# A 31-tap depthwise convolution: from VectorE taps to fp32 matrix products in four column groups

## The chip, the cores and the metric

The kernel runs on one core of one Trainium2 chip. The metric is the time of one execution on the device in microseconds (us), lower is better. The engines are called by the names that the profile uses: PE is TensorE's matrix products and PEld its weight loads, DVE is VectorE, ACT is ScalarE, POOL is GpSimd, and SP issues most of the DMAs. Each engine works through its instructions in the order in which they stand in its own queue.

## The reference

One layer of a hybrid diffusion backbone over T = 1024 tokens of width D = 1024. A modulated norm and one input projection give the inputs of four head groups of 256 channels: a Conformer convolution, a Fourier mixing (FNet), a neighbourhood attention and a state space model (SSM). Their outputs are normed, joined and projected, and a squared-ReLU MLP follows. Only the convolution is touched here:

```python
def conformer_conv(u, w_dw, b_dw, ln_g, ln_b, w_pw, b_pw):
    a, g = jnp.split(u, 2, axis=-1)
    v = a * jax.nn.sigmoid(g)
    v = lax.conv_general_dilated(v, w_dw[:, None, :], window_strides=(1,),
        padding=[(CONV_WIDTH // 2, CONV_WIDTH // 2)],   # 31 taps, 15 each side
        dimension_numbers=("NWC", "WIO", "NWC"),
        feature_group_count=D_GROUP) + b_dw             # 256 channels, one filter each
    v = jax.nn.silu(layernorm(v, ln_g, ln_b))
    return v @ w_pw + b_pw
```

## The kernel before

Everything is fp32. Most products split both factors in a high and a low part and take three products of them; the split of a tile is one ACT copy (`..h`) and one subtraction on DVE or POOL (`..l`). Activations lie with channels on the 128 partitions and tokens along the row, so that the 256 channels of the convolution are two blocks m = 0, 1 of 128, and the 1024 tokens two halves hf of H = 512 columns, one PSUM tile each.

The stages in time are: norms and modulation, the input projection with the SSM (to about 270 us), then a mixed stage to 400 us, the attention (from 400 us, 32 units to about 580), and the MLP to the end. The mixed stage holds the projection tiles of the convolution and of the queries (`x_tile`, 24 products of 512 columns each, L364), the SSM's output gate (GLU, `og` and `oa`), the FNet (`pz`, `pp`, `pq`, `fo`) and the group norms of their outputs (`pa` sums on PE, a square root and reciprocal `rc` on ACT and DVE, `pb` broadcasts on PE). The scheduler orders each engine's queue there. In the attention PE's order is written out by hand (`manual_schedule`): for each unit n the transposes of its probabilities (`p_t`, L1258), the scores of unit n + 2 (`p_s`, L1239 to L1242), from n = 4 on six steps of output-projection work (`fill(FILL)`), and the value products of unit n - 1 (`p_t`, L1270). Between `p_s` and `p_t` of a unit lie a DVE reduction (`pr`, L1244), an exponential on ACT (L1246) and, for the values, a copy on ACT (`ptt`). DVE and ACT take on these and all other work in the order that the scheduler gives.

The convolution itself: `conv_in(m)` makes the gated input in `cv` with 15 zeros on each side. `tap_steps(m, hf)` then makes one half of one block: of the 31 taps, seven are ACT scalings whose products POOL adds (`pacc`, L1013), 24 run on DVE, the first as a scaling with the bias (L1007), 23 as multiply and add (`cacc`, L1015), and a last DVE addition joins the two sums (L1018). The two halves of block 0 are called ahead of the attention, except the last two steps; those of block 1 are handed out inside it, nine steps a unit (`fill(TAPS, tps)`).

Of the kernel before, what the change touches and what calls it, by code (L numbers as in the profile page):

```python
# [8 lines left out]
F32 = mybir.dt.float32  # L9
# [8 lines left out]
P = 128  # L18
# [5 lines left out]
TWO_PI = 6.2831845  # L24
PI_ = 3.14159225
NQ = 190

COLS = {}
_n = 0
for _name, _w in (("b_mod", 48), ("g_mix", 8), ("g_mlp", 8), ("b_out", 8),  # L30
                  ("b_ff2", 8), ("g_group", 8), ("w_dw", 62), ("b_dw", 2),
                  ("ln_g", 2), ("ln_b", 2), ("b_pw", 2), ("b_fnet", 2), ("b_glu", 4),
                  ("ssm_d", 8), ("are", 16), ("aim", 16), ("cc", 16), ("g_final", 8), ("b_ff1", 32)):
    COLS[_name] = (_n, _w)
    _n += _w
# [1 line left out]
CST = {}  # L37
_n = 0
for _name, _w in (("ident", 128), ("bdc", 128), ("bds", 128), ("nidx", NQ), ("sel", 2), ("idk", 16),
                  ("rowm", 24), ("colm", 96)):  # L40
    CST[_name] = (_n, _w)
    _n += _w
NCST = _n
# [6 lines left out]
def body(tc, A, out, dbg=None):  # L50
# [60 lines left out]
    def C(name, i=0, n=1):  # L111
        o, w = COLS[name]
        return cols[:, o + i:o + i + n]
# [157 lines left out]
    kb = dram.tile([16, 16, 15, 16], F32, name="kb")  # L271
    ys_d = dram.tile([256, 8, P], F32, name="ys_d")
    yg_d = dram.tile([2, 2, P, T], F32, name="yg_d")

    st = ExitStack()
    p1 = open_pool("p1", "left", stack=st)
# [486 lines left out]

    cs = ExitStack()
    cp = open_pool("conv", "left", stack=cs)
    vs = []
    for m in range(2):
        v = cp.tile([P, T + 30], F32, name=f"cv{m}")
        V.memset(v[:, 0:15], 0.0)
        V.memset(v[:, T + 15:T + 30], 0.0)  # L770
        vs.append(v)
    wdw = cp.tile([P, 62], F32, name="wdw")
    V.tensor_scalar(wdw, C("w_dw", 0, 62), 0.5, None, ALU.mult)

    def conv_in(m):
        w = load_w(A["w_in"][2 + m])
        gth = [cp.tile([P, H], F32, name="cth", tag="csq", bufs=2) for _ in range(2)]
        for hf in range(2):
            S.activation(gth[hf], x_tile(w, hf), AF.Tanh, scale=0.5)
        w = load_w(A["w_in"][m])  # L780
        for hf in range(2):
            V.scalar_tensor_tensor(vs[m][:, 15 + hf * H:15 + (hf + 1) * H], gth[hf], 1.0, x_tile(w, hf),
                                   ALU.add, ALU.mult)

    sh = open_pool("shared", "left", stack=cs)
    ka = open_pool("keys", "left", stack=cs)
    gl = ExitStack()
    gp = open_pool("glu", "left", stack=gl)
    q4 = lambda name, dt=F32: sh.tile([P, T], dt, name=name, tag="q4", bufs=9)
    norms = []  # L790
    conv_in(0)

# [29 lines left out]
        norms.append((3, ths, [yg_d[1, m, :, sl] for m in range(2)]))  # L822
    for a_ in norms[-2:]:
        group_norm_d(gp, *a_)


    fwr = gp.tile([P, 2, 256], F32, name="fwr", tag="gsq", bufs=2)
# [163 lines left out]
    prep_bias(2)  # L991
    for jc in (0, 1, 3):
        bias(4 + jc)

    NP_TAPS = 7
    accs = [None, None]

    def tap_steps(m, hf):
        if hf == 0:
            accs[m] = cp.tile([P, T], F32, name="cacc", tag="c4", bufs=2)  # L1000
        o_ = hf * H
        acc = accs[m][:, o_:o_ + H]
        w = lambda k: wdw[:, m * 31 + k:m * 31 + k + 1]
        x = lambda k: vs[m][:, o_ + k:o_ + k + H]
        pacc = cp.tile([P, H], F32, name="pacc", tag="csq", bufs=2)
        S.activation(pacc, x(0), AF.Copy, scale=w(0))
        V.tensor_scalar(acc, x(NP_TAPS), w(NP_TAPS), C("b_dw", m), ALU.mult, ALU.add)  # L1007
        done = 1
        for n, k in enumerate(range(NP_TAPS + 1, 31)):
            if done < NP_TAPS and done * (30 - NP_TAPS) <= n * NP_TAPS:  # L1010
                t = cp.tile([P, H], F32, name="ptmp", tag="csq", bufs=2)
                S.activation(t, x(done), AF.Copy, scale=w(done))  # L1012
                G.tensor_tensor(pacc, pacc, t, ALU.add)  # L1013
                done += 1
            V.scalar_tensor_tensor(acc, x(k), w(k), acc, ALU.mult, ALU.add)  # L1015
            yield
        assert done == NP_TAPS
        V.tensor_tensor(acc, acc, pacc, ALU.add)  # L1018
        yield


    mods(1)
    for _ in tap_steps(0, 0):
        pass
    tap01 = tap_steps(0, 1)
    LATE, LD, H1 = 2, 1, 0
    for _ in range(31 - NP_TAPS - LATE):
        next(tap01)
    hps.close()


# [251 lines left out]
        yield from w_steps(0, 0)  # L1283
        yield from w_steps(2, 0)

    def taps():
        for hf in range(2):
            yield from tap_steps(1, hf)

    def mod_steps():  # L1290

        for i in range(mod_state[0], 32, 2):
# [24 lines left out]
    GL = {19: (3, 1, (0,)), 21: (3, 1, (1,)), 23: (1, 1, (0,)), 25: (1, 1, (1,))}  # L1317
    w_order = [2 * g + q for g in (3, 1, 0, 2) for q in range(2)]
    w_next = []
    bulk, tps = bulk_steps(), taps()  # L1320
    chains = {0: ln_steps(0), 1: ln_steps(1), 2: na_steps(0), 3: mod_steps()}
    TAPS = 9
    plan = {n: [] for n in range(NU)}
    for c, at in enumerate((LN0, LN1, NA0, MOD)):
        for n in at:
# [26 lines left out]
    with tc.manual_schedule(engines={mybir.EngineType.PE}):  # L1352
        scores(0)
        scores(1)
        with tc.issue_after(state["min", H1]):
            prep_head(1)
        with tc.issue_after(state["min", 1]):
            for _ in range(LATE):
                next(tap01)
        for q in range(8):  # L1360
            if LG[q] < 0:
                lead(q)
        w_next.append(load_w(A["w_out"][w_order.pop(0)]))
        for n in range(NU):
            with tc.issue_after(state["min", min(n + LD, NU - 1)]):
                for q in range(8):
                    if LG[q] == n:
                        lead(q)
            fill(TAPS, tps)
            transposes(n)  # L1370
            if n + 2 < NU:
                scores(n + 2)
            if n >= START:
                fill(FILL)
            if n > 0:
# [448 lines left out]
    return np.ascontiguousarray(v.reshape(-1, P).T)  # L1824


def ssm_d(d):
    o = np.zeros((2, 2, 32, 8), np.float32)
    o[:, :, :16] = d.reshape(8, 2, 16).transpose(1, 2, 0)
    return o.reshape(P, 8)  # L1830


def prep(inp):
# [21 lines left out]
        "b_mod": _colv(a["b_mod"][0]), "g_mix": _colv(a["g_norm_mix"][0]), "g_mlp": _colv(a["g_norm_mlp"][0]),  # L1855
        "g_final": _colv(a["g_final"]), "b_out": _colv(a["b_out"][0]), "b_ff1": _colv(a["b_ff1"][0]),
        "b_ff2": _colv(a["b_ff2"][0]), "g_group": _colv(a["g_group"][0]),
        "w_dw": a["conv_w_dw"][0].T.reshape(2, P, 31).transpose(1, 0, 2).reshape(P, 62),
        "b_dw": _colv(a["conv_b_dw"][0]), "ln_g": _colv(a["conv_ln_g"][0]), "ln_b": _colv(a["conv_ln_b"][0]),
        "b_pw": _colv(a["conv_b_pw"][0]), "b_fnet": _colv(a["fnet_b"][0]), "b_glu": _colv(a["ssm_b_glu"][0]),  # L1860
        "ssm_d": ssm_d(a["ssm_d"][0]),
# [16 lines left out]
def shape_constants():  # L1878
    c = {}
    k = np.arange(64)  # L1880
    ang = 2 * np.pi * ((k[:, None] * k[None, :]) % 64) / 64
    bd = np.zeros((2, P, P))
    for i in range(2):
        s = slice(64 * i, 64 * i + 64)
        bd[0, s, s] = np.cos(ang) / 256
        bd[1, s, s] = np.sin(ang) / 256
    nidx = np.zeros((P, NQ))
    nidx[:64] = np.arange(NQ)
    nidx[64:] = NQ - 1 - np.arange(NQ)
    sel = np.zeros((P, 2))  # L1890
    for q in range(4):
        for v in range(2):
            sel[32 * q + v, v] = 1
    idk = np.zeros((P, 16))
    for q in range(4):
        idk[32 * q:32 * q + 16] = np.eye(16)
    rowm = np.full((8, 16, 2, 12), 1e30)
    colm = np.full((8, 16, 3, 32), 1e30)
    for rh in range(2):
        for r in range(8):  # L1900
            r0 = min(max(8 * rh + r - 4, 0), 8) - 4 * rh
            rowm[r, :, rh, r0:r0 + 8] = 0
    for jc, (q0, kc0) in enumerate(((0, 0), (16, 8), (48, 32))):
        for cq in range(16):
            c0 = min(max(q0 + cq - 8, 0), 48) - kc0
            colm[:, cq, jc, c0:c0 + 16] = 0
    c["cst"] = np.concatenate([np.eye(P), bd[0], bd[1], nidx, sel, idk, rowm.reshape(P, 24), colm.reshape(P, 96)], axis=1)


    d = np.zeros((4, 2, P, 256))  # L1910
    tk = np.arange(256).reshape(2, P, 1)
    for i in range(2):
        n = 2 * tk + i
# [21 lines left out]
```

## Time and profile before

| what | value |
|---|---|
| three runs, median (lowest to highest) | 1340.45 us (1339.1 to 1341.78) |
| the profiled execution, own time | 1341.13 us |
| its span in the trace | 1339.0 us |
| mean granted TensorE clock | 0.947 of full speed |
| PE busy | 1197.4 us (89%) |
| DVE busy | 1068.4 us (80%) |
| POOL busy | 808.6 us (60%) |
| ACT busy | 652.7 us (49%) |

The span is the part of the execution that the trace covers, and 2.1 us lie around it. Busy shares are means over the stages. All times below are us from the start of the span.

### The profile page before, as it was taken

The numbers are of one execution on the slowest core, as the hardware profiler recorded it, in microseconds if no ns is written. First come the engines' busy times: TensorE is split into PE (matmuls) and PEld (weight loads), VectorE is DVE, ScalarE is ACT, GpSimd is POOL, SyncE is SP. The second block draws the span as 40 slices with busy tenths as digits, with TensorE's granted clock in tenths as the row PEclk, the third lists the DMA queues.
The fourth block names the chain that finished last, engine by engine and source line by source line (L and its number), as shares of the span: only waits on it lengthen the run. The fifth ranks groups of instructions, "written<-read, shape, count | busy, mean of one in ns | idle before, by whom it ended". The sixth has DMA issues, their size and how long they took to land.

```text
span 1339.0 us, 18718 instructions
## 1 busy us (share of the span) xinstructions
PE 1197.4 (89%) x6188; PEld 965.5 (72%) x6188; DVE 1068.4 (80%) x1636; ACT 652.7 (49%) x1337; POOL 808.6 (60%) x1002
## 2 busy tenths in 40 slices
PE   5889878898865999899999999999999999999996
PEld 3657656777655777777778777777877777777775
DVE  4775999869999768658695579888888888888867
ACT  5254333323446565554664445555545555444555
POOL 3825677372556734015367477777877778787754
PEclk9989898998975999898999999999999999999998
DMA  9455232161153544323121121111211112211113
GB/s 344 142 164 164 81 125 79 47 199 66 51 177 94 175 128 142 109 78 143 32 77 43 40 64 32 48 56 56 63 56 32 52 52 63 64 41 39 56 40 126
DMA packets 75058, 121.77 MB, mean 91 GB/s; under 512 B 16977, under 2 KB 35154, under 8 KB 74962
## 3 DMA queue, kind: packets, MB, share of 16 engines
q1 hardware_dynamic: 62802, 113.24, 26.9%
q10 hardware_dynamic: 12160, 7.34, 1.8%
q8 instruction: 49, 0.80, 0.3%
q14 instruction: 47, 0.39, 0.1%
HBM read 106.68 MB, written 13.88 MB: 90 GB/s over the span
## 4 chain that ended last, share of the span: by engine, by line
PE 48%; DVE 29%; ACT 5%; issue 4%; POOL 4%; DMA 3%; SPq 1%; ACTq 0%; DVEq 0%; POOLq 0%
PE fa L1472 11%; PE qa L1472 6%; PE qb L1472 5%; PE fb L1472 5%; DVE cacc L1015 5%; DVE tl L1488 3%; PE fc L1472 2%; DVE fl L1488 2%; PE f L1472 2%; PE p_t L1270 2%; PE mm L1097 2%; PE mm L1472 2%; DVE Ss L698 2%; DVE Ss L697 1%; DVE X L1493 1%
## 5 line engine op out<-in xcount | busy, mean ns | idle before, releaser
L1456 POOL TENSOR_TENSOR w2l<-w2r,w2h 128x128 fp32r<-128x128 f32 (+1 forms) x232 | 177.4, 766 | 75.3 <-ACT w2h L1455 68.1
L1493 DVE SCALAR_TENSOR_TENSOR X<-fa,gt2c,X 128x512 f32<-128x512 f32 x216 | 159.4, 745 | 13.0 <-PE fa L1472 13.0
L1455 ACT ACTIVATE w2h<-w2r 128x128 fp32r<-128x128 f32 (+1 forms) x232 | 85.8, 387 | 150.8 <-POOL w2r L1706 79.8
L1456 POOL TENSOR_TENSOR w2l<-w1r,w2h 128x256 fp32r<-128x256 f32 x136 | 108.5, 814 | 57.7 <-ACT w2h L1455 34.0
L235 POOL TENSOR_TENSOR wlo<-wraw,whi 128x1024 fp32r<-128x1024 f32 x30 | 75.2, 2508 | 102.0 <-ACT whi L233 82.9
L1493 DVE SCALAR_TENSOR_TENSOR X<-fb,gt2c,X 128x512 f32<-128x512 f32 x108 | 80.5, 745 | 35.4 <-PE fb L1472 35.3
L1456 POOL TENSOR_TENSOR w2l<-ws,w2h 128x256 fp32r<-128x256 f32 x84 | 67.9, 815 | 41.4 <-ACT w2h L1455 40.1
L1015 DVE SCALAR_TENSOR_TENSOR cacc<-cv,wdw,cacc 128x512 f32<-128x512 f32 x92 | 92.3, 1047 | 0.6
L364 PE MATMUL mm<-xl,whi 128*128 128x512 f32 x192 | 81.2, 424 | 3.8 <-DVE xl L220 3.8
L364 PE MATMUL mm<-xh,whi 128*128 128x512 f32 x192 | 77.3, 423 | 7.0 <-ACT xh L218 5.8
L1472 PE MATMUL fa<-th,w2h 128*128 128x512 f32 x156 | 63.2, 405 | 19.7 <-DVE X L1493 19.7
L364 PE MATMUL mm<-xh,wlo 128*128 128x512 f32 x192 | 80.6, 420 | 0.0
L1455 ACT ACTIVATE w2h<-w1r 128x256 fp32r<-128x256 f32 x136 | 53.9, 409 | 47.5 <-DVE w1r L1609 16.5
L1472 PE MATMUL qa<-cb,w2h 128*128 128x512 f32 x224 | 70.7, 397 | 0.7 <-ACT ft L1624 0.7
L1488 DVE TENSOR_TENSOR fl<-ft,fh 128x512 fp32r<-128x512 f32 x64 | 56.9, 906 | 12.8 <-ACT fh L1487 12.7
L1472 PE MATMUL fa<-th,w2l 128*128 128x512 f32 x156 | 61.7, 396 | 0.6 <-POOL w2l L1456 0.6
L1472 PE MATMUL fa<-tl,w2h 128*128 128x512 f32 x156 | 61.5, 394 | 0.0
L1013 POOL TENSOR_TENSOR pacc<-pacc,ptmp 128x512 f32<-128x512 f32 x24 | 37.4, 1559 | 29.8 <-ACT ptmp L1012 29.8
L1455 ACT ACTIVATE w2h<-ws 128x256 fp32r<-128x256 f32 x84 | 33.1, 410 | 42.4 <-DVE ws L1605 20.4
L1472 PEld LDWEIGHTS fa<-th,w2h 128*128 128x128 f32 x156 | 29.3, 188 | 30.8 <-DVE X L1493 25.2
L364 PEld LDWEIGHTS mm<-xh,whi 128*128 128x128 f32 x192 | 38.1, 201 | 18.4 <-ACT xh L218 7.2
L1472 PEld LDWEIGHTS qa<-cb,w2h 128*128 128x128 f32 x224 | 42.0, 188 | 11.2 <-ACT ft L1624 1.1
(788 smaller groups left out, 3945.3 us busy)
## 6 DMA issues: line engine op xcount, KB each, us to landing
w2r<-in_w_ff SPq DMA_DIRECT2D x68, 256.0 KB
wmB<-in_wmodB SPq DMA_DIRECT2D x32, 512.0 KB
w1r<-in_w_ff SPq DMA_DIRECT2D x64, 256.0 KB
wm<-in_wmodA SPq DMA_DIRECT2D x16, 512.0 KB
wraw<-in_w_in SPq DMA_DIRECT2D x12, 512.0 KB
x<-in_xT SPq DMA_DIRECT2D x8, 512.0 KB
wraw<-in_w_out SPq DMA_DIRECT2D x8, 512.0 KB
kr<-k_d SPq DMA_DIRECT2D x16, 256.0 KB
```

Source lines behind the costliest of these rows:

```text
L235: (lo_eng or G).tensor_tensor(lo, raw, hi.bitcast(F32), ALU.subtract)
L364: PE.matmul(o, a_[:, k, :], b_[hf][k], start=k == 0 and i == 0, stop=k == 7 and i == 2)
L698: V.tensor_tensor_scan(Ss[b_, i, g, ::-1], r_[b_], src[b_, g, ::-1], 0.0, ALU.mult, ALU.add)
L1013: G.tensor_tensor(pacc, pacc, t, ALU.add)
L1015: V.scalar_tensor_tensor(acc, x(k), w(k), acc, ALU.mult, ALU.add)
L1097: PE.matmul(o, a_[:, 2 * kk + c, :], b_, start=c == 0 and i == 0, stop=c == 1 and i == 2)
L1270: PE.matmul(po[:, j * 64:j * 64 + 64], ptt[:, i * P:(i + 1) * P], rv, start=i == 0, stop=i == 4, skip_group_check=True)
L1455: S.activation(hi, a, AF.Copy)
L1456: G.tensor_tensor(lo, a, hi.bitcast(F32), ALU.subtract)
L1472: PE.matmul(o, a_[:, i, :], m_, start=start and j == 0, stop=stop and j == 2, skip_group_check=True)
L1488: V.tensor_tensor(lo, t, hi.bitcast(F32), ALU.subtract)
L1493: return V.scalar_tensor_tensor(x, o, gt2(k), x, ALU.mult, ALU.add).ins
```

## The change

The taps leave DVE, ACT and POOL. `conv_in(m)` writes the gated input into a tile without padding and stores it to DRAM (`vv_d`, a row of 1056 floats for each channel, whose ends four small DMAs fill with zeros). `conv_taps(m)` reads it back in tiles of 256 tokens (`cvs`, two buffers): four DMAs a tile, one for each q of four groups of 32 channels, each of which puts 32 channels by four shifts of one token on the 128 partitions, 284 columns wide (145 KB). Eight products with the tap weights then cover 32 taps (the 32nd weighs zero), moving on four columns each time, and write the 32 channels of group q to column group q of the array and the 32 PSUM partitions behind it. Weights are a [128, 32] matrix for each product (`cw`), spread from a column of taps by one POOL multiplication with a mask for each m. One ACT instruction for each half adds the bias while it copies PSUM to `cacc`.

In all there are 2 stores of 512 KB, 32 loads of 145 KB, 8 tiles, 256 products of 32x256 fp32 and 4 evictions. `conv_taps(0)` is called behind the group norm of the GLU, `conv_taps(1)` right ahead of the attention; the nine tap steps a unit are gone. The host lays out the tap weights and the mask.

```diff
     def conv_in(m):
...
         w = load_w(A["w_in"][m])
+        v = q4("cv")
         for hf in range(2):
-            V.scalar_tensor_tensor(vs[m][:, 15 + hf * H:15 + (hf + 1) * H], gth[hf], 1.0, x_tile(w, hf),
-                                   ALU.add, ALU.mult)
+            V.scalar_tensor_tensor(v[:, hf * H:(hf + 1) * H], gth[hf], 1.0, x_tile(w, hf), ALU.add, ALU.mult)
+        SP.dma_start(vv_d[m * P:(m + 1) * P, 15:15 + T], v)
+    def conv_taps(m):
+        w = q4("cw").rearrange("p (a b) -> p a b", b=32)
+        G.tensor_tensor(w, C("w_dw", 32 * m, 32)[:, :, None].to_broadcast([P, 32, 32]),
+                        K("cmask")[:, None, :].to_broadcast([P, 32, 32]), ALU.mult)
+        accs[m] = cp.tile([P, T], F32, name="cacc", tag="c4", bufs=2)
+        for hf in range(2):
+            o = (at_tile, st_tile)[hf]("cw")
+            for c in range(2):
+                t0 = hf * H + c * CN
+                x = cp.tile([P, 4, CN + 28], F32, name="cvs", tag="cvs", bufs=2)
+                for q in range(4):
+                    SP.dma_start(x[:, q, :], ap(vv_d, (m * P + 32 * q) * VW + t0, [[VW, 32], [1, 4], [1, CN + 28]]))
+                for a in range(8):
+                    for q in range(4):
+                        PE.matmul(o[32 * q:32 * q + 32, c * CN:(c + 1) * CN], w[:, q * 8 + a, :], x[:, q, 4 * a:4 * a + CN],
+                                  start=a == 0, stop=a == 7, skip_group_check=True)
+            S.activation(accs[m][:, hf * H:(hf + 1) * H], o, AF.Identity, bias=C("b_dw", m))
...
         group_norm_d(gp, *a_)
+    conv_taps(0)
...
     mods(1)
-    for _ in tap_steps(0, 0):
-        pass
-    tap01 = tap_steps(0, 1)
-    LATE, LD, H1 = 2, 1, 0
-    for _ in range(31 - NP_TAPS - LATE):
-        next(tap01)
+    conv_taps(1)
+    LD, H1 = 1, 0
...
-        with tc.issue_after(state["min", 1]):
-            for _ in range(LATE):
-                next(tap01)
...
-            fill(TAPS, tps)
             transposes(n)
```

PE's queue behind the GLU (`oa`), ahead of the FNet's `pz`, in the changed kernel:

```order
966 L367 MATMUL mm<-xh,whi 128x512
967 L805 MATMUL cw<-cvs,cw 32x256 x23
968 L184 MATMUL pa<-invc,gsq 128x1 x4
969 L805 MATMUL cw<-cvs,cw 32x256 x20
970 L196 MATMUL pb<-ident,rc 128x128 x4
971 L805 MATMUL cw<-cvs,cw 32x256 x24
972 L876 MATMUL pz_3127<-cst,fu 1x128
973 L805 MATMUL cw<-cvs,cw 32x256 x2
974 L184 MATMUL pa<-invc,gsq 128x1 x4
975 L805 MATMUL cw<-cvs,cw 32x256 x22
976 L196 MATMUL pb<-ident,rc 128x128 x4
977 L805 MATMUL cw<-cvs,cw 32x256 x37
```

The 128 products of block 0 stand there nearly together, with two group norms between them and no projection tile (`mm`) to step in; before, `mm` products stood there. At the start of the attention PE's queue was this before:

```order
1143 L364 MATMUL mm<-xl,whi 128x512
1144 L183 MATMUL pa<-invc,gsq 128x1 x4
1145 L195 MATMUL pb<-ident,rc 128x128 x4
1146 L1239 MATMUL p_s<-kh,qq 128x384
1147 L1240 MATMUL p_s<-kl,qq 128x384
```

and is this after the change (line numbers are those of the changed kernel):

```order
1145 L196 MATMUL pb<-ident,rc 128x128 x4
1146 L367 MATMUL mm<-xh,whi 128x512
1147 L367 MATMUL mm<-xl,whi 128x512
1148 L367 MATMUL mm<-xh,wlo 128x512
1149 L367 MATMUL mm<-xh,whi 128x512
1150 L367 MATMUL mm<-xl,whi 128x512
1151 L367 MATMUL mm<-xh,wlo 128x512
1152 L805 MATMUL cw<-cvs,cw 32x256 x128
1153 L1230 MATMUL p_s<-kh,qq 128x384
```

The norm's broadcast `pb` has moved ahead of the last projection products, and the 128 products of block 1 stand directly ahead of the first scores. SP's queue in the changed kernel, where it comes to the last loads of block 1 (`cvs`):

```order
91 L1283 DMA wmB<-in_wmodB 128x1024
92 L982 DMA kr<-k_d 64x1024 x2
93 L984 DMA qq<-q_d 64x512 x2
94 L982 DMA kr<-k_d 64x1024 x2
95 L984 DMA qq<-q_d 64x512 x2
96 L261 DMA yg_d<-yf 128x512 x2
97 L1044 DMA X<-in_xT 128x2x512 x4
98 L1067 DMA graw<-yg_d 128x8x64
99 L802 DMA cvs<-vv_d 128x1x284 x4
100 L1129 DMA pwr<-in_w_pw 128x512
101 L1067 DMA graw<-yg_d 128x8x64
102 L802 DMA cvs<-vv_d 128x1x284 x4
```

The store of block 1 and the loads of its first two tiles stand just ahead of these rows, and before the FNet's outputs (`yf`); the loads of the third and the fourth tile stand behind the residual's loads (`X`, four of 512 KB) and behind one load of normed outputs (`graw`) each.

## Rows read from the trace of the kernel before

**Rows 1.** The page: engine totals, and the chain that ended last by line.

```profile
PE 1197.4 (89%) x6188; PEld 965.5 (72%) x6188; DVE 1068.4 (80%) x1636; ACT 652.7 (49%) x1337; POOL 808.6 (60%) x1002
...
PE fa L1472 11%; PE qa L1472 6%; PE qb L1472 5%; PE fb L1472 5%; DVE cacc L1015 5%; DVE tl L1488 3%; PE fc L1472 2%; DVE fl L1488 2%; PE f L1472 2%; PE p_t L1270 2%; PE mm L1097 2%; PE mm L1472 2%; DVE Ss L698 2%; DVE Ss L697 1%; DVE X L1493 1%
```

**Rows 2.** The page, costliest groups: busy us, mean ns, idle before.

```profile
L1015 DVE SCALAR_TENSOR_TENSOR cacc<-cv,wdw,cacc 128x512 f32<-128x512 f32 x92 | 92.3, 1047 | 0.6
...
L1013 POOL TENSOR_TENSOR pacc<-pacc,ptmp 128x512 f32<-128x512 f32 x24 | 37.4, 1559 | 29.8 <-ACT ptmp L1012 29.8
```

**Rows 3.** Stretches: busy us (instructions) per engine, PEclk, DMA share, GB/s.

```profile
290.00:400.00 110.00, 90.06 (x404) 73.41 (x403) 108.09 (x138) 44.01 (x67) 50.01 (x29) 0.89 0.32 106
400.00:434.00 34.00, 19.83 (x109) 17.98 (x108) 33.45 (x42) 19.94 (x33) 22.95 (x17) 0.55 0.39 107
...
460.00:533.00 73.00, 65.74 (x500) 57.55 (x501) 54.10 (x115) 40.83 (x78) 30.04 (x25) 0.98 0.47 139
390.00:400.00 10.00, 2.21 (x14) 2.12 (x14) 9.90 (x11) 6.59 (x11) 6.58 (x4) 0.61 0.95 308
```

**Rows 4.** TensorE's timeline from 404: transposes opening units 0, 4, 5, 6, 9, 23.

```profile
405.18 0.77 PE L1258 MATMUL p_t<-ident,pr__3571 128*128 128x128 f32 x5 [2.51 <-ACT pr__3571 L1246]
...
434.21 1.33 PE L1258 MATMUL p_t<-ident,pr__3756 128*128 128x128 f32 x5
...
439.89 0.77 PE L1258 MATMUL p_t<-ident,pr__3799 128*128 128x128 f32 x5 [0.74 <-DVE yna L1277]
...
443.95 0.74 PE L1258 MATMUL p_t<-ident,pr__3860 128*128 128x128 f32 x5
...
460.59 1.33 PE L1258 MATMUL p_t<-ident,pr__4014 128*128 128x128 f32 x5 [0.86 <-DVE yna L1277]
...
533.21 0.71 PE L1258 MATMUL p_t<-ident,pr__4748 128*128 128x128 f32 x5
```

**Rows 5.** TensorE's timeline from 389 to 401: start us, us, instruction, [idle <-releaser].

```profile
389.49 0.40 PE L364 MATMUL mm<-xh,wlo 128*128 128x512 f32 x1
389.73 0.94 PE L183 MATMUL pa<-invc,gsq 128*128 128x1 f32 x8
398.46 2.07 PE L195 MATMUL pb<-ident,rc 128*128 128x128 f32 x8 [7.79 <-DVE rc L188]
400.19 0.67 PE L1239 MATMUL p_s<-kh,qq 128*128 128x384 f32 x1
```

**Rows 6.** VectorE's timeline at the start of attention.

```profile
394.60 1.21 DVE L248 TENSOR_TENSOR kl<-kr,kh 128x1024 fp32r<-128x1024 f32 x1
...
417.72 3.59 DVE L1047 TENSOR_SCALAR X<-X,gb 128x512 f32<-128x512 f32 x3
421.23 2.18 DVE L248 TENSOR_TENSOR gl<-graw,gh 128x512 fp32r<-128x512 f32 x1
423.32 2.31 DVE L248 TENSOR_TENSOR kl<-kr,kh 128x1024 fp32r<-128x1024 f32 x1
```

**Rows 7.** TensorE's timeline, the gate vector's products, at half and at full clock.

```profile
22.49 1.94 PE L149 MATMUL pg<-wm,sT 128*32 128x256 f32 x16
...
54.67 1.07 PE L149 MATMUL pg<-wm,sT 128*32 128x256 f32 x16
55.67 1.67 PE L364 MATMUL mm<-xh,whi 128*128 128x512 f32 x6
```

**Rows 8.** TensorE's timeline, FNet: full-width products of 256 columns.

```profile
325.46 1.03 PE L874 MATMUL pp<-dft,Z 128*128 128x256 f32 x4
326.42 0.69 PE L877 MATMUL pp<-zz 1*128 1x256 f32 x2
```

**Rows 9.** The chain from 280 to 300, and from 404 to 412: loads landing.

```profile
285.53 5.47 DMA ysb<-ys_d
...
405.86 4.51 DMA qq<-q_d
```

**Rows 10.** SP's queue from 386 to 397: start us, us, line, DMA.

```profile
392.93 2.46 SPq L1053 DMA_DIRECT2D X<-in_xT  x4
```

More of the change, by code (lines that the diff above doesn't have):

```diff
@@ L26 @@
 NQ = 190
+CN = 256
 COLS = {}
@@ L30 @@
 for _name, _w in (("b_mod", 48), ("g_mix", 8), ("g_mlp", 8), ("b_out", 8),
-                  ("b_ff2", 8), ("g_group", 8), ("w_dw", 62), ("b_dw", 2),
+                  ("b_ff2", 8), ("g_group", 8), ("w_dw", 64), ("b_dw", 2),
                   ("ln_g", 2), ("ln_b", 2), ("b_pw", 2), ("b_fnet", 2), ("b_glu", 4),
@@ L39 @@
 for _name, _w in (("ident", 128), ("bdc", 128), ("bds", 128), ("nidx", NQ), ("sel", 2), ("idk", 16),
-                  ("rowm", 24), ("colm", 96)):
+                  ("rowm", 24), ("colm", 96), ("cmask", 32)):
     CST[_name] = (_n, _w)
@@ L273, in body @@
     yg_d = dram.tile([2, 2, P, T], F32, name="yg_d")
+    VW = T + 32
+    vv_d = dram.tile([256, VW], F32, name="vv_d")
     st = ExitStack()
@@ L765, in body @@
     cp = open_pool("conv", "left", stack=cs)
-    vs = []
+    accs = [None, None]
+    zp = cp.tile([P, 2, 17], F32, name="zp")
+    V.memset(zp, 0.0)
     for m in range(2):
[L768 to L773, printed above, removed]
+        for c0, n in ((0, 15), (T + 15, 17)):
+            SP.dma_start(vv_d[m * P:(m + 1) * P, c0:c0 + n], zp[:, m, 0:n])
+    sh = open_pool("shared", "left", stack=cs)
+    q4 = lambda name, dt=F32: sh.tile([P, T], dt, name=name, tag="q4", bufs=9)
     def conv_in(m):
@@ L780, in conv_in @@
         w = load_w(A["w_in"][m])
+        v = q4("cv")
         for hf in range(2):
-            V.scalar_tensor_tensor(vs[m][:, 15 + hf * H:15 + (hf + 1) * H], gth[hf], 1.0, x_tile(w, hf),
-                                   ALU.add, ALU.mult)
-    sh = open_pool("shared", "left", stack=cs)
+            V.scalar_tensor_tensor(v[:, hf * H:(hf + 1) * H], gth[hf], 1.0, x_tile(w, hf), ALU.add, ALU.mult)
[17 more added lines that the diff above has]
+            S.activation(accs[m][:, hf * H:(hf + 1) * H], o, AF.Identity, bias=C("b_dw", m))
     ka = open_pool("keys", "left", stack=cs)
@@ L788, in body @@
     gp = open_pool("glu", "left", stack=gl)
-    q4 = lambda name, dt=F32: sh.tile([P, T], dt, name=name, tag="q4", bufs=9)
     norms = []
@@ L993, in body @@
         bias(4 + jc)
[L995 to L1019, printed above, removed]
-    mods(1)
-    for _ in tap_steps(0, 0):
-        pass
-    tap01 = tap_steps(0, 1)
-    LATE, LD, H1 = 2, 1, 0
-    for _ in range(31 - NP_TAPS - LATE):
-        next(tap01)
+    mods(1)
+    conv_taps(1)
+    LD, H1 = 1, 0
     hps.close()
@@ L1284, in bulk_steps @@
         yield from w_steps(2, 0)
-    def taps():
-        for hf in range(2):
-            yield from tap_steps(1, hf)
     def mod_steps():
@@ L1319, in body @@
     w_next = []
-    bulk, tps = bulk_steps(), taps()
+    bulk = bulk_steps()
     chains = {0: ln_steps(0), 1: ln_steps(1), 2: na_steps(0), 3: mod_steps()}
-    TAPS = 9
     plan = {n: [] for n in range(NU)}
@@ L1824, in _colv, with conv_w @@
     return np.ascontiguousarray(v.reshape(-1, P).T)
+def conv_w(w):
+    o = np.zeros((32, 256), np.float32)
+    o[:31] = w
+    return o.reshape(8, 4, 2, 4, 32).transpose(4, 1, 2, 3, 0).reshape(P, 64)
 def ssm_d(d):
@@ L1857, in prep @@
         "b_ff2": _colv(a["b_ff2"][0]), "g_group": _colv(a["g_group"][0]),
-        "w_dw": a["conv_w_dw"][0].T.reshape(2, P, 31).transpose(1, 0, 2).reshape(P, 62),
+        "w_dw": conv_w(a["conv_w_dw"][0]),
         "b_dw": _colv(a["conv_b_dw"][0]), "ln_g": _colv(a["conv_ln_g"][0]), "ln_b": _colv(a["conv_ln_b"][0]),
@@ L1906, in shape_constants @@
             colm[:, cq, jc, c0:c0 + 16] = 0
-    c["cst"] = np.concatenate([np.eye(P), bd[0], bd[1], nidx, sel, idk, rowm.reshape(P, 24), colm.reshape(P, 96)], axis=1)
+    cmask = np.repeat(0.5 * np.eye(32), 4, axis=0)
+    c["cst"] = np.concatenate([np.eye(P), bd[0], bd[1], nidx, sel, idk, rowm.reshape(P, 24), colm.reshape(P, 96), cmask], axis=1)
     d = np.zeros((4, 2, P, 256))
```

## The prediction

> **What bounds the kernel now.** I read the page first. PE is busy for 89% of the span, DVE for 80%, and nearly all of the chain that ended last belongs to the MLP (`fa`, `qa`, `qb`, `fb` at L1472) [rows 1]. The taps own one entry of 5% there, `DVE cacc L1015`, and that is some 67 us of chain for 92.3 us of taps on DVE; the 24 additions on POOL cost another 37.4 us [rows 2]. So the taps are not a side work that is hidden; the question is what PE would do in their place. Next the stretches [rows 3]. From 290 to 400 us DVE is full (108.09 of 110), but PE is not far from it: 90.06 of 110, at a mean granted clock of 0.89. Ahead of the attention there are thus only 110 - 90.06 = 19.9 us in which PE is idle. From 400 to 434 DVE is full again (33.45 of 34), PE works 19.83, at a clock of 0.55. From 460 to 533, when the taps are over, PE is busy 65.74 of 73 at 0.98. That is the bound of the attention without taps.
>
> The timeline of the attention's transposes gives the same in units [rows 4]. Unit 0 opens at 405.18 and unit 4 at 434.21, 29.0 us for four units or 7.3 each. Units 4 to 9 take 434.21 to 460.59, 5.3 each, and units 9 to 23 take 72.6 us, 5.2 each. From unit 4 on, taps or none, a unit costs the same, since the projection steps fill PE. So only the first units have room. Last, the entry to the attention [rows 5]: the last projection product starts at 389.49, but `pb` waits 7.79 us for `rc`, a reciprocal of 128x4 that stands in DVE's queue among taps, and the first score starts at 400.19.
>
> **What the change removes.** 92.3 us of DVE, 37.4 us of POOL and the ACT scalings that feed it [rows 2]. With DVE free, the norm's wait of 7.79 us ends [rows 5], and the first units lose the taps that stand between their reductions, with the slow forms beside them: in the jam three `X` took 3.59 us and `kl` 2.31 [rows 6], where the same `kl` took 1.21 at 394.60 [rows 6]. `X`, `gl` and `kl` themselves stay on DVE, so the jam is thinned, not gone.
>
> **What the change adds on PE.** The gate vector's products have the very shape of the new ones, 128x256 on a [128, 32] weight in four column groups: 16 from 54.67 to the next product at 55.67, 62.5 ns each, weight loads included, at full clock [rows 7]. At 22.49 the same 16 took 1.94 us, nearly twice as long, at the lower of the clock's two levels (1.2 and 2.4 GHz): 121 ns each [rows 7]. A product on all 128 columns with as many moving columns takes (326.42 - 325.46)/4 = 240 ns at full clock [rows 8]. I take 62.5 ns, the row of the same shape: 256 x 0.0625 = 16.0 us, half of it in each block. The ends are 0.121 (31 us) and 0.240 (61 us).
>
> PE before did 90.06 us at 0.89 between 290 and 400, which is 80 us of full rate. With 16 added that is 96: without a gap the first score would start at 290 + 96 = 386. The gaps decide.
>
> **The gaps: tiles that are read back.** There are two buffers for four tiles of each block. The loads of the third wait for the last product of the first, are issued by SP and land. An issue costs some 0.6 us (four `X` in 2.46 us) [rows 10], so four take 2.4; loads of this stage landed after 4.51 (128 KB) and 5.47 us (512 KB) [rows 9]; I take 5. Tile 1 gives PE 32 x 0.0625 = 2.0 us in that time. So PE stands for 2.4 + 5 - 2.0 = 5.4 us ahead of the third tile, and about 0.4 ahead of the fourth: 5.8 us a block, where SP is free at once. It is not. In block 0 the reload stands behind loads of modulation weights and the FNet's inputs, in block 1 behind `X`, whose four loads of 512 KB are 2.1 MB, or some 7 us at the 308 GB/s of the fullest stretch [rows 3], and behind `graw`. Upper ends are thus 5.8 + 5 = 11 for block 0 and 5.8 + 7 = 13 for block 1, together 12 to 24. I take 15, since part of the queue ahead will have passed while PE works the first two tiles. That puts the first score at 386 + 15 = 401, against 400.19: **+1 us**. The stage takes in a tap work of 130 us on other engines and gives nothing back, as PE was nearly full there and now works and waits more.
>
> What is queued behind the waits: in block 0 the FNet's products, so that `yf`, `X` and the reload of block 1 come later by the same amount; in block 1 the scores, and with them everything.
>
> The store of 512 KB and the loads of the first two tiles lie behind GLU products in block 0, and behind the FNet's and the queries' products in block 1. Uncovered they would cost 5 + 4.8 + 5 = 15 us a block. The POOL spread of weights and the ACT evictions (an ACT instruction on 128x512 where 28 scalings were) are hidden: both engines lose more than they get. The attention's conv norms come from unit 4 on, some 35 us behind the eviction.
>
> **The attention.** From the first score to the fifth transposes it was 434.21 - 400.19 = 34.0 us [rows 4, 5]. Without taps, at 5.2 a unit and 5.0 from the first score to the first transposes, it is 25.8: 8.2 less. At the best spacing that the trace shows, 443.95 - 439.89 = 4.06 [rows 4], it is 21.2: 12.8 less. I take **-9.5**, nearer the first, since `X`, `gl` and `kl` stay and the clock there was 0.55. What follows is shifted, not changed.
>
> **Sum.** 1341.13 of the profiled execution (0.7 above the median of 1340.45) + 1 - 9.5 = 1332.6; I say **1332.5**.
>
> One rule of the skill gives another sum. By the Trainium skill, "DMA: Bandwidth & Descriptors", section "Anatomy of one DMA — SWDGE (gpsimd) path", the fixed share of a DMA is about 2 us; an estimate from it is a landing of about 2.5 us for 145 KB, gaps of 3 us a block and a time near 1324. The rows of this stage, 4.51 and 5.47 us, speak against it.
>
> **The rivals.** Within 0.2% (2.7 us) is about what this measurement cannot tell from no change.
>
> *More comes back (0.20).* The reloads wait 12 and the units run at 4.06: 386 + 12 - 400.2 = -2, and -12.8: 1326; with landings half as long, 1320. For it: DVE is nearly empty at 400. Against it: the clock of 0.55.
>
> *Nothing comes back (0.10).* The gaps cost 24: the first score at 410, +10, and -9.5: 1341.5. For it: the reload of block 1 stands behind `X` and `graw`. Against: part of that queue has passed.
>
> *Slower by SP's queue (0.10).* A late tile's loads wait on SP behind instructions which themselves wait for PE (block 0 for the FNet's, block 1 for `yf`), so that each gap breeds the next one: 18 a block, 36 in all, the first score at 422, +22 - 9.5: 1354. It decides when the gaps pass 15 + 8.5 + 2.7 = 26 us. Against it: the queue's waits that I can follow end before.
>
> *Slower by the clock (0.08).* Each block is two bursts of 4 us and of 2 us with a wait between. Between 290 and 400 the clock fell where PE waited (mean 0.89), and at the start of the attention it was 0.55 [rows 3]. If all products run at half clock, 121 ns: 256 x 0.0585 = +15, 1347.5. The Trainium skill, "TensorE: Matmul & The Clock Gate", section "HAM oscillation — how this bites in real kernels", describes exactly such bursts, shorter than the DMA wait for the next slice, each of which starts cold; by this rule the added products run mostly at the lower level and the time is that of this rival. The trace bears out only that clock falls with waits.
>
> *Groups not side by side (0.04).* At 240 ns a product 61 us instead of 16: 1377. It decides from (16 + 8.5)/256 = 0.096 us on. Against it: the gate vector's rows.
>
> **Chances and range.** The forecast has 0.48, and its own range is 1328 to 1337 (gaps of 12 to 19, -8.2 to -12.8). With the rival of more it makes faster 0.68. The rival of nothing and 0.03 of the clock's, where only a part of the products is slow, make 0.13 within 0.2%; what is left makes slower 0.19. The range of 1320 to 1348 takes in the clock and leaves out the queue's rival, the groups and the far end of more, under 0.2.
>
> **What would show it.** Right: `cw` products about 62 ns apart; a gap of 4 to 8 us ahead of the third tile of each block that ends on a `cvs` load; first score at 397 to 405; first units at 4.5 to 5.5 us each; the MLP as long as before. Wrong: products 120 ns apart, scores later than 410, or units that stay at 7 us, which would mean that `X`, `gl` and ACT held them and not the taps.

## The result, and the profile after

The changed kernel is slower: 1353.16 us median of four runs (1349.04 to 1356.37) against 1340.94 us of the kernel before beside it, a ratio of 1.0092 (95% interval 1.0066 to 1.0118). The forecast was 1332.5, with a range that ended at 1348. The profiled execution took 1356.37 us, the slowest of the four, with a span of 1354.6. The page's engine totals and the chain by line:

```profile
PE 1225.3 (90%) x6700; PEld 979.4 (72%) x6700; DVE 965.8 (71%) x1532; ACT 637.0 (47%) x1311; POOL 772.2 (57%) x980
...
PE fa L1454 10%; PE qa L1454 6%; PE qb L1454 5%; PE fb L1454 5%; DVE tl L1470 2%; PE cw L805 2%; PE mm L367 2%; PE mm L1088 2%; PE fc L1454 2%; PE p_t L1261 2%; DVE fl L1470 2%; PE f L1454 2%; PE mm L1454 2%; PE p_t L1249 1%; DVE X L1475 1%
```

DVE lost 102.6 us of work, as it should, and `DVE cacc` is gone from the chain [rows 1]. PE got 27.9 us and 512 instructions more, where the change adds 256 products. The stretches up to the first score, from there to the fifth transposes, and from there to the 32nd and last:

```profile
290.00:421.20 131.20, 117.44 (x913) 85.00 (x911) 35.53 (x53) 39.94 (x60) 35.73 (x22) 0.95 0.52 157
421.20:444.36 23.16, 16.56 (x106) 15.33 (x107) 19.52 (x31) 14.19 (x24) 12.39 (x9) 0.67 0.25 71
444.36:593.67 149.31, 134.06 (x979) 118.89 (x976) 91.01 (x199) 77.16 (x145) 45.72 (x35) 0.91 0.42 125
```

Ahead of the first score DVE is now nearly empty (35.53 of 131.20), PE is full, and that score starts at 421.20 instead of 400.19 [rows 3, 5]: 21.0 us later. The first four units take 23.2 us instead of 34.0, 10.9 less, so that the fifth transposes come 10.2 us late. By the last transposes (593.67 against 577.16) it is 16.5, and the span is 15.6 longer. The products on PE's timeline, a wait in block 0 with the records behind it, the last long run of block 0 with the start of the next work, and block 1:

```profile
319.58 1.53 PE L184 MATMUL pa<-invc,gsq 128*128 128x1 f32 x8 [2.30 <-DVE gsq L257]
321.04 4.49 PE L805 MATMUL cw<-cvs,cw 128*32 128x256 f32 x40
...
335.33 4.29 PE L805 MATMUL cw<-cvs,cw 128*32 128x256 f32 x73
339.24 0.38 PE L876 MATMUL pz<-cst,fu 128*1 128x128 f32 x2
...
396.66 7.11 PE L805 MATMUL cw<-cvs,cw 128*32 128x256 f32 x128
409.96 10.46 PE L805 MATMUL cw<-cvs,cw 128*32 128x256 f32 x128 [6.19 <-DMA cvs<-vv_d]
421.20 0.44 PE L1230 MATMUL p_s<-kh,qq 128*128 128x384 f32 x1 [0.78 <-ACT cacc L807]
```

Block 1 shows 2 x 128 records for 128 products. A record takes 53.5 ns at full clock (from 335.33 to 339.24, 3.91 us for 73), so a product takes 107 ns. PE worked the first two tiles of block 1 in 7.11 us, waited 6.19 for the third, and did the last two in 10.46 with a part at the clock's lower level (the granted clock was 0.50 from 409.9 to 415 and 1.00 from 416 on). In block 0 it never waited for a tile. There it waited 2.30 us for the squares of a group norm (`gsq`, on DVE), and the 40 records behind took 4.42 us up to the next work at 325.46, at a granted clock of 0.50. SP's queue in block 1:

```profile
398.34 2.74 SPq L1044 DMA_DIRECT2D X<-in_xT  x4
401.12 0.69 SPq L1067 DMA_DIRECT2D graw<-yg_d  x1
401.91 4.77 SPq L802 DMA_DIRECT2D cvs<-vv_d  x4
```

The third tile's loads were issued from 401.91 on, behind `X` and one `graw` [rows 10], took 4.77 us to issue, and landed 8.0 us after the first issue; the DMA engines moved 352 GB/s from 403.8 to 409.9. The wait in SP's queue itself was short: by an estimate (64 records of 53.5 ns from 396.66 on) the buffer was free at 400.1, 1.8 us ahead of the first issue.

### The profile page after: what moved, and what is told of

It is laid out like the page before. It is cut to its first block, busy times and chain, and to the rows that moved or that the text cites. A ratio compares the mean times of both kernels' runs of the same rounds, so it can differ in the third digit from the quotient of the medians.

```text
span 1354.6 us, 19661 instructions
## 1 busy us (share of the span) xinstructions
PE 1225.3 (90%) x6700; PEld 979.4 (72%) x6700; DVE 965.8 (71%) x1532; ACT 637.0 (47%) x1311; POOL 772.2 (57%) x980
## 4 chain that ended last, share of the span: by engine, by line
PE 52%; DVE 16%; DMA 5%; ACT 4%; issue 2%; POOL 1%; SPq 1%; DVEq 0%; ACTq 0%; POOLq 0%
PE fa L1454 10%; PE qa L1454 6%; PE qb L1454 5%; PE fb L1454 5%; DVE tl L1470 2%; PE cw L805 2%; PE mm L367 2%; PE mm L1088 2%; PE fc L1454 2%; PE p_t L1261 2%; DVE fl L1470 2%; PE f L1454 2%; PE mm L1454 2%; PE p_t L1249 1%; DVE X L1475 1%
## 5 line engine op out<-in xcount | busy, mean ns | idle before, releaser
L1437 ACT ACTIVATE w2h<-w1r 128x256 fp32r<-128x256 f32 x136 | 53.9, 409 | 46.8 <-DVE w1r L1591 16.5
L234 ACT ACTIVATE whi<-wraw 128x1024 fp32r<-128x1024 f32 x30 | 31.7, 1056 | 46.1 <-PE mm L367 14.6
L367 PEld LDWEIGHTS mm<-xh,whi 128*128 128x128 f32 x192 | 37.1, 195 | 15.6 <-ACT xh L219 6.4
L367 PEld LDWEIGHTS mm<-xl,whi 128*128 128x128 f32 x192 | 37.6, 196 | 13.8 <-DVE xl L221 3.8
```

The source lines that it names most:

```text
L234: S.activation(hi, raw, AF.Copy)
L367: PE.matmul(o, a_[:, k, :], b_[hf][k], start=k == 0 and i == 0, stop=k == 7 and i == 2)
L1437: S.activation(hi, a, AF.Copy)
```

## The experiments

Three places in the profiled execution of each run, and the granted clock of the last stretch (units 4 to 31, 979 or 980 PE records in each):

| run | first score | fifth transposes | last transposes | last stretch | clock there |
|---|---|---|---|---|---|
| before | 400.19 | 434.21 | 577.16 | 142.95 | 0.96 |
| changed | 421.20 | 444.36 | 593.67 | 149.31 | 0.91 |
| e1_half | 400.64 | 429.49 | 575.17 | 145.68 | 0.94 |
| e3_poolq | 413.17 | 436.69 | 579.56 | 142.87 | 0.96 |
| e4_noreload | 406.94 | 430.65 | 584.46 | 153.81 | 0.91 |
| e5_units | 397.21 | 432.76 | 584.76 | 152.00 | 0.92 |
| e6_bf16 | 397.19 | 418.02 | 566.61 | 148.59 | 0.93 |
| e7_thin | 397.35 | 422.90 | 574.74 | 151.84 | 0.93 |
| e8_floor | 374.58 | 395.72 | 541.95 | 146.23 | 0.96 |
| e9_thin2 | 381.53 | 405.10 | 578.02 | 172.92 | 0.88 |
| e10_bf16b4 | 389.36 | 410.62 | 553.94 | 143.32 | 0.96 |
| e11_bf16u | 387.49 | 411.85 | 562.77 | 150.92 | 0.91 |
| e12_pool_hi | 417.64 | 441.06 | 586.19 | 145.13 | 0.96 |
| e13_before_pool_hi | 401.51 | 436.34 | 590.48 | 154.14 | 0.91 |

The theory after the result was that a product costs twice what I had counted, on a PE that had no room for it (price theory). The rival was that the reloads set the pace (wait theory).

**e1_half**: half of the products.

```diff
-                for a in range(8):
+                for a in range(4):
...
-                                  start=a == 0, stop=a == 7, skip_group_check=True)
+                                  start=a == 0, stop=a == 3, skip_group_check=True)
```

> Half of the added products: only four of the eight shift groups, 128 products instead of 256 (16 of the 32 taps are left out, loads unchanged). Price theory (a product is two passes of some 54 ns, 107 ns in all, on a PE that has no room ahead of the attention): 13.7 us less on PE, first score at about 407 instead of 421, time about 1340 where the changed kernel has 1353. Wait theory (the late reloads set the pace, products fit beside them): tiles still arrive when they did, first score no more than 5 us earlier, time 1348 or more.

Measured: 1336.86 us, ratio to before 0.998 (0.9962 to 0.9998), 16.3 us below the changed kernel. The first score came 20.6 us earlier, more than the 13.7 of the products alone: the wait ahead of the third tile also fell, from 6.19 us to 2.31, and the burst behind it was shorter. PE then waited 5.7 us for an exponential (`pr`) in the first units, so that 14.9 us of the lead were left at the fifth transposes. The wait theory's bound of 5 us falls. PE's timeline, block 1:

```profile
388.12 3.66 PE L805 MATMUL cw<-cvs,cw 128*32 128x256 f32 x64
394.09 5.77 PE L805 MATMUL cw<-cvs,cw 128*32 128x256 f32 x64 [2.31 <-DMA cvs<-vv_d]
400.64 0.45 PE L1230 MATMUL p_s<-kh,qq 128*128 128x384 f32 x1 [0.78 <-ACT cacc L807]
```

**e3_poolq**: the loads on POOL's queue.

```diff
-                    SP.dma_start(x[:, q, :], ap(vv_d, (m * P + 32 * q) * VW + t0, [[VW, 32], [1, 4], [1, CN + 28]]))
+                    G.dma_start(x[:, q, :], ap(vv_d, (m * P + 32 * q) * VW + t0, [[VW, 32], [1, 4], [1, CN + 28]]))
```

> All loads of tiles are issued from POOL's queue instead of SP's, everything else unchanged. Wait theory: the reloads of block 1 no longer stand behind the four residual loads and a load of normed outputs, the wait of 6 us ahead of the third tile and the slow last half disappear, first score 8 to 12 us earlier, time 1342 to 1346. Price theory: only that wait of some 6 us is to be had, 2 to 6 us, time 1347 to 1351; less if POOL's own work or its way of issuing holds the loads up.

Measured: 1349.66 us (1338.61 to 1352.49), ratio 1.009 (1.0056 to 1.0123). The wait ahead of the third tile went from 6.19 to 2.20 and 1.17 us and the first score came 8.0 earlier in the profiled execution, but the median fell by only 3.5 us, and by the ratio hardly at all. The first score moved as the wait theory said, the median as the price theory said. The profiled execution was the fastest of four that lie 14 us apart, so this run alone decides nothing. Of the 8.0 us, 4.8 were there when block 1 began (391.83 against 396.66).

**e4_noreload**: two tiles a block, used for both halves.

```diff
-                x = cp.tile([P, 4, CN + 28], F32, name="cvs", tag="cvs", bufs=2)
-                for q in range(4):
-                    SP.dma_start(x[:, q, :], ap(vv_d, (m * P + 32 * q) * VW + t0, [[VW, 32], [1, 4], [1, CN + 28]]))
+                if hf == 0:
+                    xs.append(cp.tile([P, 4, CN + 28], F32, name="cvs", tag="cvs", bufs=2))
+                    for q in range(4):
+                        SP.dma_start(xs[c][:, q, :], ap(vv_d, (m * P + 32 * q) * VW + t0, [[VW, 32], [1, 4], [1, CN + 28]]))
+                x = xs[c]
```

> Each block loads two tiles only and uses them for both halves (the second half is computed from the first half's input; number and kind of products unchanged). Price theory: the products stay, 27 us at full clock, only the gaps ahead of the third and fourth tile go: first score at about 410, 8 to 11 us earlier, time 1343 to 1346. Wait theory: all of the loss goes, first score at 400 or before, time 1332 or less.

Measured: 1342.18 us, ratio 1.0021 (1.0002 to 1.0040). The first score came 14.3 us earlier. PE's timeline shows block 1 without a gap, 256 records from 392.11 to 406.13 at full clock, 54.8 ns each, and the first score behind its eviction:

```profile
392.11 14.02 PE L808 MATMUL cw<-cvs,cw 128*32 128x256 f32 x256
406.94 0.45 PE L1233 MATMUL p_s<-kh,qq 128*128 128x384 f32 x1 [0.81 <-ACT cacc L810]
```

In block 1 the reloads, with the half clock behind them, cost 9.7 us (23.8 us from its first product to its last there, 14.0 here), within the 8 to 11 of the price theory. The other 4.6 of the 14.3 lie ahead of block 1, where PE waited for no tile in either kernel; 2.3 of them were there at the very first product (314.49 against 312.18). Executions differ by some of that: in e12_pool_hi below, with the code of the changed kernel up to there, block 1 begins at 393.82 instead of 396.66. But even without the reloads the change gains nothing: what is left uses up what the taps set free.

**e5_units**: block 1 in units 0 to 3 of the attention.

```diff
-    conv_taps(1)
...
+    TPU = 8
+    tps = unit_taps(1)
+    next(tps)
...
             if n + 2 < NU:
                 scores(n + 2)
+            if n < START:
+                fill(TPU, tps)
```

(`unit_taps` issues the same loads and products as `conv_taps`, and yields behind each four products.)

> The 128 products of block 1 are moved from ahead of the first score into units 0 to 3 of the attention (eight steps of four products after the scores of each unit), where PE waits for ACT and DVE; block 0 as in the changed kernel. Price theory: first score at 397 to 400, the four units take 27 to 30 us instead of 23, fifth transposes at 427 to 432 instead of 444, time 1339 to 1343, about that of the kernel before. Wait theory: the reloads hold the units up instead, fifth transposes not before 440, time 1350.

Measured: 1344.31 us, ratio 1.0033 (1.0018 to 1.0049). The first score came at 397.21, as expected, but the four units took 35.6 us, not 27 to 30: they waited 3.42 us for a tile, and the products ran partly at half clock. It beats the changed kernel by 8.9 us and still loses to the one before.

**e6_bf16**: input, weights and tiles in bf16.

```diff
-    vv_d = dram.tile([256, VW], F32, name="vv_d")
+    vv_d = dram.tile([256, VW], BF16, name="vv_d")
...
-        w = q4("cw").rearrange("p (a b) -> p a b", b=32)
+        w = q4("cw", BF16).rearrange("p (a b) -> p a b", b=32)
...
-                x = cp.tile([P, 4, CN + 28], F32, name="cvs", tag="cvs", bufs=2)
+                x = cp.tile([P, 4, CN + 28], BF16, name="cvs", tag="cvs", bufs=2)
```

(`zp` and `cv` likewise. The input and the taps are rounded to bf16, so precision is left out.)

> The changed kernel with the convolution's input, tap weights and tiles in bf16 (rounded to bf16, so precision is left out; number of products unchanged, loads half the bytes). Pass theory (an fp32 product runs as two passes, which I counted as one in the price of 62.5 ns): the trace shows 256 product records instead of 512, products of 54 ns or less, first score at 398 to 405 instead of 421, time 1336 to 1343. If the price hangs on columns and groups and not on passes: products stay at 107 ns, first score at 412 or later, time 1346 or more.

Measured: 1326.54 us, ratio 0.9901 (0.9872 to 0.9930): faster than before by 1%, and more than expected. The instructions of the line show one record for a product, and the timeline 64 of them in 1.93 us:

```profile
L806 PE MATMUL cw<-cvs,cw x256: 272/273/421, 316.3 to 396.0; 128*32 128x256 bf16 x128
```

```profile
385.33 1.93 PE L806 MATMUL cw<-cvs,cw 128*32 128x256 bf16 x64
390.99 3.27 PE L806 MATMUL cw<-cvs,cw 128*32 128x256 bf16 x35 [3.73 <-DMA cvs<-vv_d]
```

The same kind of line of the changed kernel:

```profile
L805 PE MATMUL cw<-cvs,cw x512: 379/379/636, 314.5 to 420.0; 128*32 128x256 f32 x171
```

The pass theory's forecast came true, one record where fp32 leaves two, and a record is also shorter than one of fp32. Loads of half the size help too, so this run alone does not part the two; with e1_half and e4_noreload it does.

**e8_floor**: no convolution at all (the spread of the tap weights goes too).

```diff
-        SP.dma_start(vv_d[m * P:(m + 1) * P, 15:15 + T], v)
...
-                    SP.dma_start(x[:, q, :], ap(vv_d, (m * P + 32 * q) * VW + t0, [[VW, 32], [1, 4], [1, CN + 28]]))
-                for a in range(8):
...
-            S.activation(accs[m][:, hf * H:(hf + 1) * H], o, AF.Identity, bias=C("b_dw", m))
+            sl = slice(hf * H, (hf + 1) * H)
+            S.activation(accs[m][:, sl], vs[m][:, sl], AF.Identity, bias=C("b_dw", m))
```

> The changed kernel without the convolution (the 31 taps are left out: the gated input plus bias takes the place of the result; no store, no loads, no products). The floor of the stage. Price theory: first score at 385 to 390, fifth transposes at 408 to 414, time 1318 to 1326, which would make the taps before cost some 15 to 20 us and the products some 30. If the later units are paced by the weight loads of the output projection, whatever comes ahead of them, a part of the lead at unit 4 is gone by unit 31 (3 to 8 us), time 1326 to 1332.

Measured: 1303.16 us, ratio 0.9733 (0.9694 to 0.9772). I had expected 1318 to 1332. The taps before cost some 37 us of time, not 15 to 20. The stretch from 290 to the first score and the one up to the fifth transposes:

```profile
374.58:395.72 21.14, 16.50 (x109) 15.28 (x108) 17.64 (x29) 14.79 (x23) 9.52 (x9) 0.68 1.04 279
...
290.00:374.58 84.58, 82.25 (x407) 67.32 (x405) 32.11 (x50) 35.85 (x55) 32.21 (x20) 1.00 0.39 125
```

PE works 82.25 of 84.58 us at full clock: without the convolution that stage is bounded by PE alone, and work put on PE there is paid for.

**e7_thin** and **e9_thin2**: the kernel before, with the last half of one block, or of both, held back behind unit 4.

```diff
-            fill(TAPS, tps)
+            if n < START:
+                fill(8 if n < 3 else 7, tps)
+            else:
+                with tc.issue_after(state["min", min(n + LD, NU - 1)]):
+                    fill(3, tps)
             transposes(n)
```

(e9_thin2 fills the first half of block 1 until unit 3, the last half of block 0 until unit 11, and the last half of block 1 behind it, four steps a unit.)

> The kernel before, taps on DVE, ACT and POOL as they were, but the last half of block 1 (hf 1, which the second norm chain needs only at unit 20) is held back to units 4 to 14, three steps a unit. Theory (the kernel before lost time where DVE was full, from 340 to 434 us, and DVE has room behind unit 4): 24 taps or 18 us leave the full stretch, first score 3 to 8 us earlier, fifth transposes at 420 to 427 instead of 434, time 1327 to 1334. Rival (behind unit 4 the taps hold the units up as they did before): what is won ahead is lost again by unit 20, 1337 to 1342.

> As the run that holds back the last half of block 1, but the last half of block 0 too: 62 steps in units 4 to 19, four a unit. If DVE has room for them behind unit 4 (54 of 73 us busy there before): first score at 386 to 392, fifth transposes at 412 to 420, time 1323 to 1330. Rival: four taps a unit (3 us of 5.2) fill DVE in the attention, units of 5.2 become 6 or more, time 1336 or more.

Measured: 1340.39 us, ratio 1.0001 (0.9982 to 1.0020), and 1343.68 us, ratio 1.0028 (0.9997 to 1.0059). Both leads were there, and both were given back. In e7_thin the fifth transposes came at 422.90, 11.3 us early, and the last ones at 574.74, 2.4 early. In e9_thin2 they came at 405.10, 29.1 early, and at 578.02. The stretch between them shows DVE busy 144.48 of 172.92, at a lower clock:

```profile
405.10:578.02 172.92, 140.19 (x979) 121.34 (x976) 144.48 (x256) 85.50 (x158) 64.05 (x45) 0.88 0.35 108
```

The rival stands: behind unit 4 taps on DVE hold the units up about as much as they did ahead of them. It is e9_thin2 that shows it; the 151.84 us of e7_thin's last stretch lie within what that stretch varies by without any taps (143 to 154 in the table), and there only the medians speak.

**e10_bf16b4** and **e11_bf16u**: bf16 with four buffers for tiles, and that with block 1 in the units.

```diff
-                x = cp.tile([P, 4, CN + 28], BF16, name="cvs", tag="cvs", bufs=2)
+                x = cp.tile([P, 4, CN + 28], BF16, name="cvs", tag="cvs", bufs=4)
```

(e11_bf16u: the edit of e5_units on top.)

> The bf16 run (input, weights and tiles of the convolution rounded to bf16) with four buffers for tiles, which its half-sized tiles allow: no load waits for a product any more. Where the reloads still held PE up in the bf16 run (3.7 us ahead of the third tile of block 1, two gaps in block 0): first score at 385 to 391 instead of 397, time 1316 to 1322 instead of 1326.5. If the gaps were hidden by other work of PE: first score no more than 3 us earlier, time 1323 to 1327.

> The bf16 run with four buffers, and the products of block 1 in units 0 to 3 of the attention (rounded to bf16 as before). If PE has room there: first score at 380 to 386, the four units as long as without products (20 to 23 us), time 3 to 6 us below the run with four buffers alone. If the units take the products on top: the same time as that run.

Measured: 1317.29 us, ratio 0.9863 (0.9807 to 0.9919), and 1320.15 us, ratio 0.9867 (0.9825 to 0.9910). e10_bf16b4 is the fastest version of the convolution here, with e11_bf16u within its noise, 1.4% below the kernel before, with the input and the taps rounded to bf16. Its block 1 has no wait for a tile:

```profile
382.83 3.68 PE L806 MATMUL cw<-cvs,cw 128*32 128x256 bf16 x128
389.36 0.45 PE L1231 MATMUL p_s<-kh,qq 128*128 128x384 f32 x1 [2.85 <-ACT cacc L808]
```

Of the 14.8 us that its first score still lies above that of e8_floor, the products are 7.4 (256 x 28.8 ns); most of the rest is waiting, 4.9 us for the norm's squares in block 0 (0.8 in e8_floor) and 2.85 for the eviction. Products in the units gained nothing more: the first score came only 1.9 us earlier and the four units took that back.

**e12_pool_hi** and **e13_before_pool_hi**: the copy for the high part of `w_out` on POOL, in the changed kernel and in the one before.

```diff
-        S.activation(hi, raw, AF.Copy)
+        if hi_eng is None:
+            S.activation(hi, raw, AF.Copy)
+        else:
+            hi_eng.tensor_copy(hi, raw)
...
-        w_next.append(load_w(A["w_out"][w_order.pop(0)]))
+        w_next.append(load_w(A["w_out"][w_order.pop(0)], hi_eng=G))
```

> The changed kernel, where the copy that makes the high part of the output projection's weights in the attention runs on POOL instead of ACT, so that ACT's exponentials and copies no longer stand behind a weight load that has not landed. Theory (behind unit 4 the changed kernel loses 0 to 7 us where ACT waits for that load, PE waits for ACT and the clock falls): units 4 to 31 in 140 to 144 us at a clock of 0.95 or more instead of 149 at 0.91, time 1343 to 1348. Rival (the late part varies by itself): time within 3 us of the changed kernel, 1350 to 1356.

> The kernel before with the same move of that copy from ACT to POOL. Theory: it has the same wait in its late units, but at a clock of 0.96 it lost little: time 1335 to 1340. Rival (ACT's wait costs every version the same): as much faster here as in the changed kernel, 6 us or more, below 1334.

Measured: 1349.01 us (1343.11 to 1357.39), ratio 1.0071 (1.0042 to 1.0101), and 1352.67 us, ratio 1.0094 (1.0064 to 1.0124). The first lies between theory and rival, the second goes against both: the kernel before became 12 us slower. PE still waited 10.0 us for ACT's `ptt` in units 4 to 31 of e12_pool_hi, at a clock of 0.96, against 7.9 at 0.91 in the changed kernel. So ACT's wait for the weight load is not what parts the late stretches.

## Why the prediction was wrong

**PE nearly full: right.** I worked out 80 us of PE work behind 290, a first score at 370 without the convolution. e8_floor gave 374.58, with PE full. The 4.6 us between are about 2 of conversion (82.25 us of work at full clock, not 80) and 2.3 in which PE waits even there.

**The price of a product: the step that failed.** "I take 62.5 ns, the row of the same shape: 256 x 0.0625 = 16.0 us." The row said x16 [rows 7], and I divided by 16. The call that it stands for has a loop of eight products; each fp32 product leaves two records. The row of the full-width products misled in the same way: its x4 [rows 8] were two products. So the price in the row was 125 ns, up to the start of the next work, and it measured 107. The 256 products take 512 x 0.0535 = 27.4 us at full clock, 11.4 more than my term. That is above the 0.096 from which the prediction's own sum turns to slower, and near its upper end of 0.121. PE's work in that stage is paid for: 13.7 us of products less (e1_half) brought 16.3 in the median. The Trainium skill, "FP8 and Floating Point Precision", section "TensorE Precision Notes", says that true fp32 takes four passes through the array. The trace shows two records, but 107 ns against the 28.8 of a bf16 product (128 in 3.68 us), 3.7 times, which is near four passes.

**The gaps: right in block 1, and right in the sum by luck.** I took 15 us, about half of it in each block, and without the reloads the first score came 14.3 us earlier (e4_noreload). In block 1 the mechanism was as I had it: 6.19 us of wait ahead of the third tile, where I had 5.4 with SP free, none ahead of the fourth, and 3.3 us more in the burst behind, most of it half clock (10.46 against 7.11). In block 0 I forecast 5.8 to 11 and PE waited for no tile. The sum with landings of some 2.5 us does not hold: the third tile landed 8.0 us after its first issue. (The figure that it took is headed as one of the GpSimd path, and these loads go out on SP.)

The Trainium skill, "TensorE: Matmul & The Clock Gate", section "HAM oscillation — how this bites in real kernels", is borne out by that one burst, which started at a granted clock of 0.50 behind its wait. The bursts as a whole did not run cold: the clock up to the first score was 0.95, above the 0.89 of before [rows 3]. The two stretches at half clock cost some 5.6 us by an estimate from the rows (4.42 against 40 x 0.0535, and 10.46 against 7.11), where the clock rival has 15, so it holds only in part.

**A term that was put at nothing.** I let PE work block 0 without a wait of its own and called the evictions hidden. But with the products there and no projection product between the norms, PE waited 2.3 us for the GLU norm's squares (0.8 in e8_floor, where projection and FNet products stand there and the norm's sums start 0.5 us later), ran at half clock behind that wait, and the last eviction held the first score up by 0.78 us.

**The first score.** Forecast 370 + 16 + 15 = 401. Measured 374.6 + 27.4 + 14.3 + 4.9 = 421.2, where 4.9 is what e4_noreload keeps above the floor beyond its products (406.94 - 374.58 - 27.4): 1.6 us more of the norm's wait, 1.7 of half clock behind it (40 records in 3.84 us), 0.8 of eviction, and some 0.8 that no row places. Of the 20 us that I missed, 11.4 are the price, 4.6 the floor, and some 4 this last term.

**The attention: right for the first units.** Forecast 9.5 us less, measured 10.9. One reading beside it was wrong: "From unit 4 on, taps or none, a unit costs the same". In the kernel before the last DVE tap starts at 414.9, in unit 1, so those units had no taps on DVE; with 46 taps put there (e9_thin2) they take 172.92 us instead of 142.95.

**What follows: not quite shifted.** Between the fifth and the last transposes the profiled execution lost another 6.4 us, at a clock of 0.91 instead of 0.96. The median run lost less, 12.2 us in all; in the profiled execution 10.2 were there at the fifth transposes.

**The rivals.** The one of SP's queue gave 422 for the first score and 1354, nearly what was measured, but not by its mechanism: it needs 36 us of gaps that breed each other, and PE waited for a tile once, for 6.19 us. With the loads off SP (e3_poolq) the first score came 8.0 us earlier in the traced execution, and the median fell by 3.5 us. Groups that do not run side by side are excluded: records in the four groups start 53.5 ns apart, where one of full width takes 240 [rows 8].

**The sum in one view.** By the fifth transposes the convolution cost 434.21 - 395.72 = 38.5 us before and 444.36 - 395.72 = 48.6 after. Ahead of the first score it went from 25.6 to 46.6, in the first units from 12.9 to 2.0. The freed 92 us of DVE were worth 10.9 us in the units and were not worth more ahead of them, where PE, with the products on it, took DVE's place as the bound.

What stays open is the late stretch. Its 979 PE records take 143 to 146 us in the executions that were granted 0.94 or more and 149 to 154 in those at 0.91 to 0.93 (without the two with taps behind unit 4), in old and new kernels alike. I found no wait that decides which it is.

## What to carry to other kernels

Before a row's time is divided by its count, set the count against the number of calls in the code: an fp32 product can be more than one record. Where work is moved onto the engine that bounds a stage, its price is paid in full, while taking it off the other engine pays only where that one was the bound; a run with the work left out shows both at once. If the target engine is the bound, the form of the work (here bf16 tiles, with buffers enough that none waits, where their rounding is allowed) decides whether the move is worth it.

## What the runs showed of the hardware that was not expected

An fp32 product of 256 columns in four column groups took 107 ns as two records, the same product in bf16 28.8 ns as one. The attention's last 28 units took 143 to 154 us with the same number of PE records, at a granted clock of 0.96 to 0.91 that differed between executions; what decides it stays open.
